# A two-layer hybrid decoder on one core: an SBUF pool for HGRN2's query and gate tiles, a smaller index branch, and pools that wait tile by tile

## The chip and the metric

The kernel runs on one core of a Trainium2 chip. The metric is device time in microseconds of one execution; of a set of runs the median counts. The engines, in the words of the profile: PE (TensorE, its weight loads as PEld), DVE (VectorE), ACT (ScalarE), POOL (GpSimd) and SP, which only issues DMAs. Each engine takes its instructions in a fixed order. On-chip memory is SBUF (128 partitions; a tile takes the same bytes in each) and PSUM (eight banks of 2 KB a partition, where matmuls accumulate).

## The reference

The input is `x` (512 tokens of 1024), a memory of 256 rows, and the weights of two layers in fp32. In each layer one projection of the normed residual (`w_in`) feeds four mixers side by side; their outputs, 256 columns each, go through `w_out` and are added to the residual. Then come cross attention to the memory and a SwiGLU FFN.

```
for l in range(2):
    h = rms_norm(x, norm_mix[l])
    c_hg, c_dsa, c_nsa, c_ml = split(h @ w_in[l])
    mixed = concat(hgrn2(c_hg), dsa(c_dsa), nsa(c_nsa), mlstm(c_ml))
    x = x + mixed @ w_out[l]
    x = x + cross_attention(rms_norm(x), rms_norm(mem))
    x = x + swiglu(rms_norm(x))
```

- HGRN2 takes queries `q`, forget gates `f`, values `i` and output gates `g` (four heads of 64) through a gated linear recurrence.
- DSA scores every key for every query with a small index branch: `score = sum over 8 heads of relu(iq . ik) * iw`. It keeps the 128 best keys of each query and attends to those with ordinary attention heads.
- NSA adds up three attentions (compressed blocks, selected blocks, a window), and mLSTM is a gated matrix memory, computed here in parallel form.

## The kernel before

**Order of the work.** All of a layer's code is emitted by Python generators. `weave` and `mix` (lines 1351 to 1367) take steps from several generators in turn, so that by the costs written in `COST` all end together; `first()` (line 245) marks instructions that go ahead of others. The program's framework then puts the instructions of each engine in an order that it chooses by a simulation of its own (line 1464), with the order of emission as the priority. So the code sets what may come early, not what does.

A layer has four stages:

1. `dsa_in` (line 538) multiplies the index columns of DSA while the residual is read row chunk by row chunk. Then `weave` runs DSA's index branch (`dsa`) beside a chain that holds `nsa_in`, `nsa`, `ml_in`, `ml`, `dsa_in2` and `hg_in`.
2. HGRN2 itself (`hg`), DSA's attention (`dsa_attn`), the projection out of the first mixers (`out_stage`) and the keys of the memory (`xa_kv`).
3. Cross attention (`xa_in`, `xa`).
4. The FFN.

**Products.** Each fp32 product is made of three: hi by hi, hi by lo, lo by hi. A weight tile is loaded by SP (`raw_tile`, line 265, three buffers `wr`), rounded to its hi on ACT (line 285) and its lo computed on POOL (line 286; six buffers each, `wh` and `wl`). `proj_T` (line 434) makes a transposed chunk of 128 columns by 512 tokens, 24 matmuls at lines 294 to 296, and evacuates it on DVE at line 438. `proj_tok` (line 441) makes blocks of 128 tokens by about 256 columns, 24 matmuls at lines 304 to 306 each, and evacuates each on ACT at line 450. Both accumulate in `acc`, two PSUM banks: a third accumulation can start only when one of the two has been evacuated.

**DSA's index branch** (lines 561 to 623). For the query blocks 1 to 3, `index(tb)` splits and transposes the queries into `iqs` and `iqT`, multiplies head by head (line 598), takes the ReLU on ACT (line 600) and adds the heads up in `iacc{tb}` on DVE (lines 603 to 607). `select(tb)` then runs 16 rounds of the eight largest and their replacement on DVE (lines 615 and 616) and writes a mask (line 619). `iqs` and `iqT` take turns in a tag of two buffers of 4 KB; each block has an `iacc` of its own.

**Pools.** Tiles live in pools, which are opened and closed like a stack, from the left and from the right of SBUF. A pool that lands on the bytes of a closed one waits for it: all its tiles wait for every user of every closed pool on those bytes. On the right lies `dsa`; when the index branch has been emitted, `hg_space` (line 687) closes it and opens `hgin` there, and `hg_in` (line 693) waits for that before it makes its tiles:

```
right.close()                                    # hg_space
self.hin = self.pool(right, "hgin", side="right")
while self.hin is None:                          # hg_in
    yield 0.5
pool = self.hin
self.h_q = self.t(pool, "h_q", [128, 2, S], bufs=1)
```

`hg_in` makes the transposed `h_q` and `h_f` (two chunks each, in the order q0, f0, q1, f1), then `h_v` and `h_g` (four blocks each). Right after, on the same side, comes `xk` with `memT`, pieces of the memory that SP loads (line 1166).

On the left lie, in the first stage, `keep` (what DSA keeps: masks, latent, queries), `ml` (mLSTM) and `nsa`. At the border to the second stage `ml` and `nsa` close, and on their bytes come the residual anew (`load_x`, `xT` from DRAM, lines 370 and following), `hg` with the tile `lvf` (line 740, first layer only), and `dat` with `wukv` (line 639), DSA's small weights. The PSUM banks besides `acc` are pools too (`ba`, `bb`, `bc` by stage).

Of the kernel before, what the change touches and what calls it, by code (L numbers as in the profile page):

```python
# [8 lines left out]
FR = mybir.dt.float32r  # L9
# [14 lines left out]
# column vectors, one column each, per layer  # L24
# [53 lines left out]
class Stream:  # L78
    """The layout of the weight stream: one flat array, tile after tile."""
# [6 lines left out]
    def tile(self, layer, name, kc, c0, c1):  # L86
        """Rows (kc chunks of 128) and columns c0:c1 of a weight -> [128, nk, c]."""
# [9 lines left out]
def pack(inp):  # L97
# [36 lines left out]
    # small weights: [w_uk | w_uv], w1 of the compressions, their w2  # L134
# [14 lines left out]
def plan(st, l):  # L149
    """Every tile of the stream of one layer in the order in which it is used."""  # L150
# [8 lines left out]
    # NSA without kc and vc  # L159
# [4 lines left out]
    tok_chunk("dsai", "w_in", DSA0 + 384, DSA0 + 680)  # L164
# [33 lines left out]
# rows of w_out by stage: HGRN2 0-1, DSA 2-3, NSA 4-5, mLSTM 6-7  # L198
# [4 lines left out]
class Kernel:  # L203
# [18 lines left out]
    # ---------------------------------------------------------------- helpers  # L222
    def psum(self, tag, shape=(128, 512), pool=None):
        """Banks by tag; the lane of a pool may have its own."""
        tag = self.alias.get(id(pool), {}).get(tag, tag)
        pool, bufs = self.pt[tag]
        return pool.tile(list(shape), FT, name=tag, tag=tag, bufs=bufs)

    def banks(self, stack, name, **tags):
        """The banks of a stage, besides those of acc."""  # L230
        pool = stack.enter_context(self.tc.tile_pool(name=f"{name}{self.l}", bufs=1, space=bass.MemoryType.PSUM))
        self.pt.update({t: (pool, n) for t, n in tags.items()})

    def t4(self, pool, name, shape, dt=FT):
        """A temporary of up to 4 KB a partition."""
        return pool.tile(list(shape), dt, name=name, tag="t4", bufs=self.nt[id(pool)][1])

    def t2(self, pool, name, shape, dt=FT):
        """A temporary of up to 2 KB a partition."""
# [5 lines left out]
    def first(self):  # L245
        """Scheduled ahead of what was emitted a while before."""
# [14 lines left out]
    def weights(self, key):  # L261
        """Loads the tiles of a chunk and splits them into hi and lo: a list by row chunk."""
        return [w for tile in self.plans[self.l][key] for w in self.weight_tile(tile)]

    def raw_tile(self, tile):
        """A tile of the stream [128, rows / 128, columns]."""
# [9 lines left out]
    def weight_tile(self, tile, pool=None):  # L276
        """Its hi and lo by row chunk; in a pool of their own if they are used for long."""
# [11 lines left out]
    def mm_T(self, acc, w, x):  # L289
        """acc[c, t] = w^T x; x by row chunk, as (hi, lo)."""  # L290
# [7 lines left out]
    def mm_tok(self, acc, w, x, tb, first=True, last=True):  # L298
        """acc[t, c] of one block of tokens."""
# [8 lines left out]
    def rsqrt(self, pool, dst, src, mul, add):  # L308
        """dst = (src * mul + add) ** -0.5, on small tiles."""
# [11 lines left out]
    def rope(self, x, c, s, half, pool, eng=None):  # L321
        """x [128, TB, H, d] in place; c, s [128, TB, 2 half]."""
# [11 lines left out]
    def sumsq(self, dst, x, pool):  # L334
        """dst [128, a(, b)] = sum of squares over the last axis of x."""
# [1133 lines left out]
```

## Time and profile before

| | |
|---|---|
| time, median of 3 runs | 1743.08 us (1739.02 to 1747.72) |
| the profiled execution, span from first to last instruction | 1744.4 us |
| PE busy | 1649.7 us, 95% |
| PEld busy | 1359.7 us, 78% |
| DVE busy | 993.2 us, 57% |
| POOL, ACT busy | 781.0 us, 712.0 us |
| mean granted clock of PE | 0.944 |

The profile gives no other time for its own execution than its span; the span lies within the runs' times. A matmul's busy time is modelled from its start to its end, and matmuls overlap, so a busy PE isn't a PE at its peak. The granted clock says at which speed PE ran: 1.00 is 2.4 GHz, 0.50 is 1.2 GHz, and a value between is a mean over a stretch. A wait names the work that ended last among what an instruction waited for. "Line" in the profile is a line of the kernel, often that of a helper, so that tiles say more than lines.

### The profile page before, as it was taken

How to read it: one execution, taken by the hardware profiler on the slowest of the kernel's cores; microseconds unless marked ns; L12 is line 12 of the kernel's file. 1: busy time of each engine (PE TensorE's matmuls, PEld its weight loads, DVE VectorE, ACT ScalarE, POOL GpSimd, SP SyncE). 2: the span in 40 equal slices, each digit the busy share in tenths (PEclk: the TensorE clock that was granted, in tenths of full speed). 3: DMA queues.
4: the chain of work that ended last, by engine and by line, in shares of the span. 5: the costliest groups of instructions: out<-in, count | busy, mean ns of one | idle time of the engine just before them, and what ended most of it. 6: DMA issues, size and time to landing. Idle time of an engine off the chain costs nothing.

```text
span 1744.4 us, 25033 instructions
## 1 busy us (share of the span) xinstructions
PE 1649.7 (95%) x9026; PEld 1359.7 (78%) x9030; DVE 993.2 (57%) x2022; ACT 712.0 (41%) x1537; POOL 781.0 (45%) x696
## 2 busy tenths in 40 slices
PE   7889899899899999999997998989998999999999
PEld 7778586677778888888896886867786888888887
DVE  5599856868774430343227997568867644214430
ACT  5455435326553322333334453452465433223321
POOL 5663232525615444444446543325464244444442
PEclk9999699959999999999998996988799999999999
DMA  5343111301503333333333321121022123333332
GB/s 155 103 117 84 37 43 37 100 13 35 171 13 97 92 93 95 96 97 91 98 96 109 95 83 43 43 75 43 22 84 84 43 91 94 89 101 96 92 101 67
DMA packets 82107, 140.38 MB, mean 80 GB/s; under 512 B 9400, under 2 KB 22456, under 8 KB 81984
## 3 DMA queue, kind: packets, MB, share of 16 engines
q1 hardware_dynamic: 79632, 133.81, 26.7%
q10 hardware_dynamic: 2032, 3.94, 0.7%
q8 instruction: 71, 1.16, 0.3%
q0 software_dynamic: 320, 1.05, 0.2%
q14 instruction: 52, 0.43, 0.1%
HBM read 134.55 MB, written 4.21 MB: 80 GB/s over the span
## 4 chain that ended last, share of the span: by engine, by line
PE 71%; DVE 19%; issue 3%; ACT 2%; POOL 2%; DMA 2%; SPq 0%; ACTq 0%; POOLq 0%; DVEq 0%
PE acc L294 12%; PE acc L295 12%; PE acc L296 12%; PE sc L295 5%; PE sc L296 5%; PE sc L294 5%; PE hb L770 3%; PE o L533 2%; DVE iacc L616 2%; PE tp L458 2%; DVE m L615 2%; PE acc L304 2%; PE acc L306 2%; PE acc L305 2%; PE mb L950 1%
## 5 line engine op out<-in xcount | busy, mean ns | idle before, releaser
L286 POOL TENSOR_TENSOR wl<-wr,wh 128x512 fp32r<-128x512 f32 (+4 forms) x496 | 623.6, 1265 | 658.0 <-ACT wh L285 624.3
L285 ACT ACTIVATE wh<-wr 128x512 fp32r<-128x512 f32 (+4 forms) x496 | 296.1, 603 | 517.4 <-PE acc L295 207.5
L294 PE MATMUL acc<-xh,wh 128*128 128x512 f32 (+1 forms) x704 | 275.6, 395 | 6.4 <-DVE xT L431 4.1
L295 PE MATMUL acc<-xl,wh 128*128 128x512 f32 (+1 forms) x704 | 274.9, 391 | 0.7 <-DVE xl L316 0.7
L296 PE MATMUL acc<-xh,wl 128*128 128x512 f32 (+1 forms) x704 | 273.8, 390 | 0.1
L431 DVE TENSOR_TENSOR xT<-acc,xT 128x512 f32<-128x512 f32 (+1 forms) x112 | 67.7, 610 | 215.8 <-PE acc L296 215.5
L294 PEld LDWEIGHTS acc<-xh,wh 128*128 128x128 f32 x704 | 133.9, 191 | 38.3 <-DVE xT L431 4.7
L295 PEld LDWEIGHTS acc<-xl,wh 128*128 128x128 f32 x704 | 134.6, 191 | 29.5 <-DVE xl L316 1.4
L296 PEld LDWEIGHTS acc<-xh,wl 128*128 128x128 f32 x704 | 134.3, 191 | 27.6 <-POOL wl L286 0.4
L304 PE MATMUL acc<-wh,xh 128*128 128x256 f32 (+2 forms) x480 | 138.0, 289 | 3.6 <-ACT h_g L450 1.3
L295 PE MATMUL sc<-xl,wh 128*128 128x512 f32 x352 | 139.6, 397 | 0.0
L296 PE MATMUL sc<-xh,wl 128*128 128x512 f32 x352 | 138.8, 394 | 0.0
L294 PE MATMUL sc<-xh,wh 128*128 128x512 f32 x352 | 138.4, 394 | 0.0
L296 PE MATMUL acc<-f_gh,wl 128*128 128x512 f32 x352 | 138.3, 395 | 0.0
L295 PE MATMUL acc<-f_gl,wh 128*128 128x512 f32 x352 | 138.1, 394 | 0.0
L294 PE MATMUL acc<-f_gh,wh 128*128 128x512 f32 x352 | 137.9, 394 | 0.0
L305 PE MATMUL acc<-wl,xh 128*128 128x256 f32 (+2 forms) x480 | 137.0, 286 | 0.0
L306 PE MATMUL acc<-wh,xl 128*128 128x256 f32 (+2 forms) x480 | 136.8, 285 | 0.0
L1329 DVE SCALAR_TENSOR_TENSOR f_b<-sc,R 128x512 f32<-128x512 f32 x44 | 30.4, 691 | 127.5 <-PE sc L296 127.5
L304 PEld LDWEIGHTS acc<-wh,xh 128*128 128x128 f32 x480 | 90.4, 189 | 6.3 <-ACT h_g L450 1.5
L305 PEld LDWEIGHTS acc<-wl,xh 128*128 128x128 f32 x480 | 90.6, 189 | 1.1 <-issue 0.6
L306 PEld LDWEIGHTS acc<-wh,xl 128*128 128x128 f32 x480 | 90.7, 189 | 0.9 <-issue 0.8
(396 smaller groups left out, 3204.4 us busy)
## 6 DMA issues: line engine op xcount, KB each, us to landing
wr<-in_wst SPq DMA_DIRECT2D x384, 256.0 KB, 2.6
wr<-in_wst SPq DMA_DIRECT2D x48, 128.0 KB, 2.6
wr<-in_wst SPq DMA_DIRECT2D x32, 192.0 KB, 2.4
wr<-in_wst SPq DMA_DIRECT2D x16, 262.0 KB, 2.7
wr<-in_wst SPq DMA_DIRECT2D x8, 296.0 KB, 3.4
wr<-in_wst SPq DMA_DIRECT2D x8, 264.0 KB, 2.8
m_Mb<-m_dram ACTq DMA_DIRECT2D x8, 256.0 KB, 3.5
memT<-in_memT SPq DMA_DIRECT2D x16, 128.0 KB, 2.1
```

The costliest lines, as they stand in the source:

```text
L285: nc.scalar.activation(hi, raw, AF.Copy)
L286: nc.gpsimd.tensor_tensor(lo, raw, hi.bitcast(FT), op=OP.subtract)
L294: self.nc.tensor.matmul(acc, wh, xh, start=(j == 0), stop=False)
L295: self.nc.tensor.matmul(acc, wh, xl, start=False, stop=False)
L296: self.nc.tensor.matmul(acc, wl, xh, start=False, stop=(j == n - 1))
L304: self.nc.tensor.matmul(acc, xh[:, s], wh, start=(first and j == 0), stop=False)
L305: self.nc.tensor.matmul(acc, xh[:, s], wl, start=False, stop=False)
L306: self.nc.tensor.matmul(acc, xl[:, s], wh, start=False, stop=(last and j == n - 1))
L431: self.nc.vector.tensor_add(self.xT[c][:, cols], acc, self.xT[c][:, cols])
L458: self.nc.tensor.transpose(p[:rows, j * 128:j * 128 + 128], src(j), self.ident)
L533: nc.tensor.matmul(o[64 * e:64 * e + 64, hp], v(sb), pT[e][:, sb * 128:sb * 128 + 128], start=(first and sb == 0), stop=(last and sb == tb ...
L770: nc.tensor.matmul(sc[s0:s1, b + t0:b + t1], kk[po:po + 64, b + s0:b + s1], qq[po:po + 64, b + t0:b + t1], start=True, stop=True)
```

## The change

- HGRN2's `h_q` and `h_f` get a pool `hgqf` of their own, opened on the right before `dsa`. `hg_in` makes them without waiting; it waits for `hgin`, which now holds `h_v` and `h_g` alone, after the four transposed chunks.
- `dsa` closes by a stack of its own (`index`).
- DSA's index branch has one `iqs`, one `iqT` and one `iacc` for all blocks. Its weights come in eight tiles of one row chunk instead of four of two, so that all weight buffers get smaller.
- Every pool that is opened by `pool`, by `banks` (PSUM), by `load_x` and by `open_sq` is opened with `reuse_waits="tile"`: a tile then waits only for the users of earlier tiles on its own bytes (in PSUM, its own bank), and not for all users of the closed pools.

Comments and docstrings that the diff takes out are left out here.

```diff
@@ plan
-    tok_chunk("dsai", "w_in", DSA0 + 384, DSA0 + 680)
+    out["dsai"] = [st.tile(l, "w_in", (k,), DSA0 + 384, DSA0 + 680) for k in range(8)]
@@ banks
-        pool = stack.enter_context(self.tc.tile_pool(name=f"{name}{self.l}", bufs=1, space=bass.MemoryType.PSUM))
+        pool = stack.enter_context(self.tc.tile_pool(name=f"{name}{self.l}", bufs=1, space=bass.MemoryType.PSUM, reuse_waits="tile"))
@@ load_x, and the same in open_sq
-        self.xp = self.xpool.enter_context(self.tc.tile_pool(name=f"xp{self.nx}", bufs=1))
+        self.xp = self.xpool.enter_context(self.tc.tile_pool(name=f"xp{self.nx}", bufs=1, reuse_waits="tile"))
@@ dsa_in
-                if c % 2 == 0:
-                    w += self.weight_tile(self.plans[self.l]["dsai"][c // 2])
+                w += self.weight_tile(self.plans[self.l]["dsai"][c])
@@ dsa, index(tb)
-            iqs = self.t4(pool, "iqs", [128, 8, 96], FR)
+            iqs = self.t(pool, "iqs", [128, 8, 96], FR, bufs=1)
...
-            iqT = self.t4(pool, "iqT", [128, 8, 128], FR)
+            iqT = self.t(pool, "iqT", [128, 8, 128], FR, bufs=1)
...
-            acc = self.t(pool, f"iacc{tb}", [128, n], bufs=1)
+            acc = self.t(pool, "iacc", [128, S], bufs=1)[:, :n]
@@ hg_space, hg_in
-    def hg_space(self, right):
-        right.close()
+    def hg_space(self, index, right):
+        index.close()
         self.hin = self.pool(right, "hgin", side="right")
...
-        while self.hin is None:
-            yield 0.5
-        pool = self.hin
+        pool = self.hqf
         self.h_q = self.t(pool, "h_q", [128, 2, S], bufs=1)
         self.h_f = self.t(pool, "h_f", [128, 2, S], bufs=1)
         for c in (0, 2, 1, 3):
             yield from self.proj_T(f"hgT{c}", (self.h_f if c > 1 else self.h_q)[:, c % 2], self.x)
...
+        while self.hin is None:
+            yield 0.5
+        pool = self.hin
         self.h_v = self.t(pool, "h_v", [128, TB, 256], bufs=1)
@@ pool
-        p = stack.enter_context(self.tc.tile_pool(name=f"{name}{self.l}", bufs=2, side=side))
+        p = stack.enter_context(self.tc.tile_pool(name=f"{name}{self.l}", bufs=2, side=side, reuse_waits="tile"))
@@ run
-            right = ExitStack()
+            right, index = ExitStack(), ExitStack()
+            self.hqf = self.pool(right, "hgqf", side="right")
...
-            pd = self.pool(right, "dsa", n2=4, n4=2, side="right")
+            pd = self.pool(index, "dsa", n2=4, n4=0, side="right")
...
-            self.weave((self.chain(self.dsa(pd, pk), self.hg_space(right)), COST["dsa"]),
+            self.weave((self.chain(self.dsa(pd, pk), self.hg_space(index, right)), COST["dsa"]),
```

## Rows read from the trace of the kernel before

**Rows 1.** Page, head and part 1: busy us, share of the span, instructions.

```profile
span 1744.4 us, 25033 instructions
...
PE 1649.7 (95%) x9026; PEld 1359.7 (78%) x9030; DVE 993.2 (57%) x2022; ACT 712.0 (41%) x1537; POOL 781.0 (45%) x696
```

**Rows 2.** Windows of the two stages: stretch, us, busy by engine, clock, DMA, GB/s.

```profile
181.00:215.20 34.20, 26.75 (x103) 19.05 (x101) 27.49 (x77) 13.24 (x41) 7.70 (x6) 0.55 0.11 32
215.20:302.00 86.80, 83.41 (x569) 66.91 (x570) 52.12 (x122) 42.67 (x108) 24.45 (x19) 0.96 0.15 43
302.00:318.40 16.40, 11.40 (x71) 8.29 (x69) 8.74 (x18) 6.66 (x13) 7.90 (x13) 0.96 0.51 169
1048.00:1077.30 29.30, 24.43 (x96) 17.81 (x95) 22.57 (x58) 9.76 (x31) 7.79 (x6) 0.55 0.15 45
1077.30:1174.10 96.80, 91.70 (x603) 73.28 (x602) 59.30 (x142) 47.17 (x118) 26.47 (x21) 0.92 0.17 48
1174.10:1183.00 8.90, 7.41 (x39) 6.37 (x39) 7.95 (x14) 4.50 (x9) 7.22 (x13) 0.69 0.32 119
```

**Rows 3.** Tiles: HGRN2's evacuations and DSA's masks, duration min/median/max, first and last start.

```profile
L438 DVE TENSOR_TENSOR h_q<-acc,R x2: 674/682/691, 215.2 to 226.6; 128x512 f32<-128x512 f32 x2
...
L450 ACT ACTIVATE h_v<-acc,r x4: 453/469/476, 240.7 to 257.5; 128x256 f32<-128x256 f32 x4
...
L450 ACT ACTIVATE h_g<-acc,rcol x4: 463/472/474, 267.5 to 277.3; 128x256 f32<-128x256 f32 x4
...
L619 DVE TENSOR_SCALAR dmask<-iacc x3: 344/412/1075, 107.4 to 214.3; 128x256 bf16<-128x256 f32 x1, 128x384 bf16<-128x384 f32 x1, 128x512 bf16<-128x512 f32 x1
...
L438 DVE TENSOR_TENSOR h_q<-acc,R x2: 680/686/691, 1077.2 to 1085.6; 128x512 f32<-128x512 f32 x2
```

**Rows 4.** Timeline of PE: start, us, instruction, [idle before <-releaser].

```profile
185.36 0.79 PE L950 MATMUL mb<-m_hi,m_hi 64*128 64x512 f32 x1 [4.09 <-ACT m_hi L919]
...
230.22 0.39 PE L295 MATMUL acc<-xl,wh 128*128 128x512 f32 x1
230.45 0.39 PE L296 MATMUL acc<-xh,wl 128*128 128x512 f32 x1
...
236.94 0.28 PE L304 MATMUL acc<-wh,xh 128*128 128x256 f32 x1
237.05 0.28 PE L305 MATMUL acc<-wl,xh 128*128 128x256 f32 x1
```

**Rows 5.** Windows of 10 us, columns as in rows 2.

```profile
150.00:160.00 10.00, 10.00 (x86) 9.60 (x85) 9.80 (x31) 5.77 (x12) 1.15 (x2) 1.00 0.07 26
290.00:300.00 10.00, 10.00 (x78) 7.30 (x72) 6.77 (x17) 6.68 (x18) 0.28 (x1) 1.00 0.01 2
610.00:620.00 10.00, 10.00 (x45) 8.10 (x44) 3.84 (x5) 3.62 (x6) 4.86 (x4) 1.00 0.37 98
1140.00:1150.00 10.00, 10.00 (x46) 8.07 (x44) 5.34 (x14) 3.31 (x10) 3.04 (x3) 0.50 0.10 33
```

**Rows 6.** Timeline of DVE: index scores of DSA's last block.

```profile
130.94 0.74 DVE L607 SCALAR_TENSOR_TENSOR iacc<-rel,d_idx,iacc 128x512 f32<-128x512 f32 x1
...
152.87 0.73 DVE L607 SCALAR_TENSOR_TENSOR iacc<-rel,d_idx,iacc 128x512 f32<-128x512 f32 x1
```

**Rows 7.** Chain at the ends of the first stages; a wait of PE.

```profile
309.76 6.67 DMA lvf<-in_levels
...
1174.14 3.62 DMA wukv<-in_wukv
...
PE acc L294 <- DVE xT L431: 3.4, 1, 3.4
```

**Rows 8.** Page, part 6: weight loads, KB each, median us to landing.

```profile
wr<-in_wst SPq DMA_DIRECT2D x8, 296.0 KB, 3.4
...
wr<-in_wst SPq DMA_DIRECT2D x48, 128.0 KB, 2.6
```

**Rows 9.** Waits of the SP queue, 150 to 260 us: total, times, longest.

```profile
SPq L1166 <- DVE dmask L619: 25.8, 1, 25.8
```

More of the change, by code (lines that the diff above doesn't have):

```diff
@@ L372, in open_sq @@
     def open_sq(self):
-        self.sq = self.xpool.enter_context(self.tc.tile_pool(name=f"sq{self.nx}", bufs=1))
+        self.sq = self.xpool.enter_context(self.tc.tile_pool(name=f"sq{self.nx}", bufs=1, reuse_waits="tile"))
     def layer_consts(self):
```

## The prediction

> **What bounds the kernel now.** I read the page first, for the one number that seems to close the case: the span is 1744.4 us and TensorE (PE) is busy for 95% of it [rows 1]. The profiled execution stands 1.3 us above the median of the runs, 1743.08 us; I make the sum against 1744.4, and this kernel's measurement can tell about 0.5% (8.7 us) from no change. PE's busy time is no proof of full work, since a matmul lasts longer at the lower clock, so I went next to the windows: where is PE busy at half speed? Of the whole kernel one kind of stretch stands out, once in each layer. In 181 to 215.2 us PE is busy 26.75 of 34.2 us at a mean granted clock of 0.55, that is mostly at 1.2 GHz; in 1048 to 1077.3 us it is 24.43 of 29.3 us at 0.55 [rows 2]. PE entered the first after 4.09 us of waiting [rows 4].
>
> Then the tiles, to see what ends the stretch. The last mask of DSA, the last reader of its index scores, starts at 214.3 us, and the first evacuation into `h_q` at 215.2 us; HGRN2's `h_v` follows from 240.7 and `h_g` from 267.5 us [rows 3]. The second layer repeats it: `h_q` first at 1077.2 us, where that stretch ends. The code says why. `hg_in` starts its projections only into tiles of the pool `hgin`, which lies on the bytes of the DSA pool and waits for all of that pool. Two transposed chunks are multiplied early into the two banks of `acc`; they can't leave, so no other projection can run, and PE has attention alone until the mask is done. VectorE (DVE) is not free then either: 27.49 of 34.2 us [rows 2].
>
> **The change, part by part.**
>
> *1. The transposed tiles get their own pool.* `h_q` and `h_f` no longer wait for DSA. Two chunks that now run after 215.2 us can run in the stretch: 2 x 24 matmuls at 0.23 us from start to start, 11.0 us [rows 4]. Behind them `hgi` and `hgg` have four blocks each, 24 matmuls at 0.12 us: 2.9 us a block. After the change `h_v` lies, by the sizes of the tiles in the code, on the index branch's `iqs` and `iqT`, and `h_g` mostly on `iqT` and `iacc`. With waits tile by tile `h_v` waits for the last index product (its scores end at 152.87 us [rows 6]), `h_g` still for the last mask. So four blocks of `hgi` (11.6 us) can leave, and two of `hgg` (5.8 us) can sit in the banks: 28.4 us of work for the stretch. The room there, as busy time at the granted clock: 34.2 - 26.75 x 0.55 = 19.5 us, and 29.3 - 24.43 x 0.55 = 15.9 us in the second layer; together 35.4 us. The supply holds: dense projections cost GpSimd 4.86 and ScalarE 3.62 per 10 us [rows 5], 16.6 and 12.4 us over the stretch, beside 7.70 and 13.24 of 34.2 already there [rows 2]. Does the freed time come off the end? The rest of the stage (215.2 to 302) is 83.41 of 86.8 us busy at 0.96, and its last ten microseconds before 300, with hardly a projection left, still have PE at 10.0 [rows 2, 5]. So the rest is bound by PE, and what leaves it shortens it. The bounds are 0 (the rest keeps its length) and 35.4. I take 30, near the upper end, because of those two rows; the deduction of 5 is one more fall of the clock like that of 1140 to 1150 us, ten microseconds at 0.50 [rows 5].
>
> The matmul's busy share would leave much less room (34.2 - 26.75 = 7.4 us in layer 0). The Trainium skill ("Perfetto Trace Analysis", Identifying the Most-Contended Engine) says that busy matmul time is a bad measure of headroom and puts the busy share of weight loads in its place. By that, as an estimate, the room is 34.2 - 19.05 / 0.81 = 10.7 us, the 0.81 being the share in a dense stretch, and 7.3 us in the second layer; the sum of this part would be 18 us and not 30. The trace agrees on the first half: busy share and clock differ as above.
>
> *2. Pools wait tile by tile.* At the first stage's end all tiles of the next wait for all of NSA and mLSTM. In layer 0 the chain then goes through the load of `lvf`, 6.67 us from 309.76, and PE waits 3.4 us for the residual; in layer 1 through the load of `wukv`, 3.62 us at 1174.14 [rows 7]. `wukv` lands on tiles of the compression that were done long before, so its wait goes: 3.6 us. Of the eight residual tiles the last lie on `m_tok`, which is read to the end, but no longer hold the others back: I take the 3.4 us. Room: 16.4 - 11.40 x 0.96 = 5.5 and 8.9 - 7.41 x 0.69 = 3.8 us [rows 2], so 0 to 9.3; I take 7. At the other borders the chain shows no wait for a pool: 0. The addresses of the PSUM banks change nothing but the same border.
>
> *3. One `iacc` instead of three.* The scores of a block now follow the selection before them. In layer 0 the last block's accumulation spread over 130.94 to 152.87 us, between the rounds of that selection [rows 6]; run after it, DSA can end up to 22 us later for each of two blocks. DSA's end is not the stage's: 214.3 + 44 = 258 us is still before 302. What hides it is NSA's and mLSTM's work on DVE, 9.80 of 10 us in 150 to 160 [rows 5]. Price 0. If that cover is gone, up to 22 us of DVE work moves into a rest of 86.8 - 19.5 = 67.3 us that holds 52.12 already [rows 2]: 74 us, 7 too many in each layer, 14 in all. That is the bound.
>
> *4. DSA's weights row chunk by row chunk.* Four loads of 296 KB become eight of half that, with four more splits on ScalarE and GpSimd; `iqs` and `iqT` alternated in two buffers and now have one each, which is the same order. A load of 128 KB takes 2.6 us to land against 3.4 [rows 8], so the fourth tile of layer 0 can be 2 us late, as three buffers now hold three row chunks and not six; the first product can be as much as 1.5 us earlier. Layer 1 has them under the FFN's dense PE. Price 0, bounds -1.5 and +2. The Trainium skill ("DMA: Bandwidth & Descriptors", Rules for kernel authors) advises to coalesce small transfers, which speaks against this part. The trace agrees in kind, with the two times to landing above, and gives it no more than those 2 us.
>
> Sum: 30 + 7 = 37 us; 1744.4 - 37 = 1707 us.
>
> **The rivals.**
>
> *The tail stays.* NSA and mLSTM are chains of dependent steps; if the rest is bound by them and not by PE, the projections move and the end does not. Against it: PE at 10.0 of 10 in 290 to 300 [rows 5]. For it: at this clock some of that is waiting inside the chain. Only part 2 is left: 1737 us.
>
> *DVE becomes the bound*, as worked out in part 3: 14 us given back, 1721 us.
>
> *Less room*: weight loads fill the stretch more than the clock lets one think, 18 us instead of 30: 1719 us, by the row of the weight loads [rows 2]. This is the rule of the Trainium skill named under part 1.
>
> *The borders give more.* The whole 35.4 and 9.3 us, and half of what the rests of the stages leave (86.8 - 83.41 x 0.96 = 6.7 and 96.8 - 91.70 x 0.92 = 12.4 us [rows 2]): 54 us, 1690 us.
>
> *Slower: a load blocks the weight queue.* SP issues in order. Today it stands 25.8 us at a load of `memT` that waits for DSA's mask [rows 9], with weights behind it, and nobody minds, since projections are stopped too. With finer waits such loads are placed earlier, into the time in which projections run at their densest. Six split tiles and three raw ones, about 2.8 us of PE each (12 matmuls x 0.23), cover 25 us; a stand of 45 us would cost 20 us of PE: 1764 us. It decides once the queue stands longer than those 25 us. Against it: the tiles under `memT` will be free when the index products end, long before the mask.
>
> *The change does not do what it says*: the order of the instructions is chosen by a scheduler, and if it keeps the projections where they are, the time stays at 1744 us.
>
> **How the numbers follow.** Forecast 0.48; tail stays 0.12; DVE 0.09; less room 0.05; borders give more 0.15; slower 0.07; not done 0.04. The predicted time is the forecast's, 1707 us. Faster by over 0.5% (below 1734.4): 0.48 + 0.09 + 0.05 + 0.15 = 0.77. Within 0.5%: 0.12 + 0.04 = 0.16. Slower: 0.07. The range runs from 1684, the deep case with a few microseconds of its own, to 1740, which takes in the staying tail; the queue's case, the unchanged one and the edges are left out, under 2 in 10.
>
> **What would show it.** Part 1: `h_q` and `h_f` evacuated in full before the last mask, `h_v` too, `h_g` just after it; the clock of that stretch near 1.0; the rest of the stage some 15 us shorter in each layer. Part 2: `lvf` and `wukv` gone from the chain. Part 3: the last mask later than 214 us, with the stage's end not following it. Part 4: the first weights in place earlier, dsa's products ending within 2 us of now. I am wrong if the stretch is filled and the stage ends where it did (the tail), if DVE is near 10 of 10 until the stage's end (part 3), or if SP shows waits of over 25 us with projections behind them.

## The result, and the profile after

The changed kernel takes 1724.93 us (median of 4 runs, 1717.81 to 1726.85), beside 1744.28 us for the kernel before in the same session: 19.4 us less, ratio 0.9896 with a 95% interval of 0.9866 to 0.9926. On a second chip it was 1726.21 against 1742.00 us, 0.9924 (0.9900 to 0.9947). It is faster, as forecast, by about half of the 37 us forecast. The profiled execution took 1724.88 us, with a span of 1723.1 us against 1744.4.

The head of the page and its part 1, against [rows 1]: TensorE (PE) is still at 95%.

```profile
span 1723.1 us, 25048 instructions
...
PE 1633.3 (95%) x9026; PEld 1347.7 (78%) x9030; DVE 989.5 (57%) x2022; ACT 712.8 (41%) x1545; POOL 793.5 (46%) x704
```

The evacuations and masks of layer 0 in the changed kernel, by tile, against [rows 3] (minimum, median and maximum duration in ns, then first and last start):

```profile
L438 DVE TENSOR_TENSOR h_q<-acc,R x2: 674/677/680, 179.2 to 193.4; 128x512 f32<-128x512 f32 x2
...
L450 ACT ACTIVATE h_v<-acc,r x4: 458/476/477, 206.6 to 219.2; 128x256 f32<-128x256 f32 x4
...
L450 ACT ACTIVATE h_g<-acc,rcol x4: 474/475/476, 224.5 to 240.3; 128x256 f32<-128x256 f32 x4
...
L618 DVE TENSOR_SCALAR dmask<-iacc x3: 294/351/406, 99.8 to 207.2; 128x256 bf16<-128x256 f32 x1, 128x384 bf16<-128x384 f32 x1, 128x512 bf16<-128x512 f32 x1
```

`h_q` leaves 36 us earlier than before, and the last projection is out at 240.3 us instead of 277.3. The stretch that stood at half clock is filled. But look at what comes behind it. These are windows of the changed kernel, with the columns of [rows 2] (stretch, its length, busy us of PE, weight loads, DVE, ACT and POOL, granted clock, DMA share, GB/s):

```profile
181.00:215.20 34.20, 33.85 (x214) 27.64 (x214) 31.24 (x83) 14.38 (x41) 13.48 (x11) 1.00 0.23 70
215.20:240.00 24.80, 24.80 (x187) 21.63 (x188) 14.37 (x37) 12.87 (x35) 6.92 (x6) 1.00 0.17 54
240.00:282.00 42.00, 33.03 (x154) 23.62 (x153) 26.73 (x57) 17.36 (x46) 11.78 (x9) 0.67 0.10 27
282.00:300.60 18.60, 17.47 (x137) 12.81 (x138) 11.29 (x33) 11.02 (x29) 2.59 (x4) 1.00 0.28 86
```

From 181 to 240 us PE is full at the upper of its two clocks (2.4 GHz). From 240, when the last projection is through, to 282 us it is at a mean of 0.67, and the windows of 10 us show how it falls: a short supply first, then half clock with PE called busy all the time.

```profile
230.00:240.00 10.00, 10.00 (x82) 8.89 (x81) 5.48 (x16) 5.35 (x14) 0.77 (x1) 1.00 0.01 2
240.00:250.00 10.00, 4.75 (x35) 3.13 (x34) 9.85 (x12) 5.99 (x15) 8.34 (x7) 0.99 0.40 111
250.00:260.00 10.00, 7.13 (x32) 5.10 (x32) 8.05 (x21) 4.55 (x12) 2.17 (x2) 0.66 0.00 0
260.00:270.00 10.00, 9.90 (x37) 6.52 (x37) 4.92 (x15) 4.34 (x13) 1.27 (x1) 0.51 0.01 2
270.00:280.00 10.00, 10.00 (x44) 7.85 (x44) 2.69 (x7) 1.82 (x5) 0.00 (x0) 0.50 0.00 0
...
1100.00:1110.00 10.00, 7.20 (x36) 4.87 (x36) 9.18 (x15) 6.20 (x15) 6.47 (x5) 0.66 0.38 111
1110.00:1120.00 10.00, 8.13 (x40) 4.75 (x40) 8.63 (x27) 7.16 (x20) 1.92 (x2) 0.84 0.00 1
```

The last two lines are about the same place in layer 1: its clock is on the way up again, at 0.84, in the second window, where layer 0 stays down for 20 us more.

For the account of the whole I cut the span into layer stages: the first stage (DSA's index, NSA, mLSTM and the projections in, to NSA's last output), the second part (HGRN2, DSA's attention, the products out and cross attention, to the next norm) and the FFN. In each, busy time times granted clock is the work at full clock, and the rest of the length I call *lost*. First the kernel before, then the changed one; the third and sixth pieces, the FFNs, lose next to nothing in either and are left out.

```profile
0.00:305.60 305.60, 269.84 (x1701) 227.84 (x1701) 220.15 (x542) 148.69 (x345) 133.10 (x116) 0.92 0.29 82
305.60:532.40 226.80, 209.28 (x1315) 171.95 (x1318) 167.07 (x357) 106.19 (x259) 103.31 (x113) 0.89 0.23 68
...
900.10:1174.10 274.00, 249.78 (x1550) 208.40 (x1548) 203.56 (x499) 129.53 (x309) 113.95 (x90) 0.90 0.25 71
1174.10:1392.40 218.30, 205.10 (x1314) 168.25 (x1317) 165.77 (x353) 105.36 (x259) 102.94 (x113) 0.91 0.20 58
```

```profile
0.00:300.60 300.60, 266.25 (x1702) 226.23 (x1703) 219.26 (x542) 149.07 (x349) 139.67 (x122) 0.94 0.30 89
300.60:524.50 223.90, 207.63 (x1314) 170.27 (x1316) 167.00 (x356) 105.90 (x259) 104.15 (x112) 0.90 0.21 59
...
892.60:1150.30 257.70, 237.00 (x1550) 198.44 (x1549) 202.55 (x499) 129.24 (x309) 117.19 (x92) 0.95 0.27 78
1150.30:1371.20 220.90, 206.37 (x1314) 169.56 (x1317) 164.69 (x355) 105.64 (x259) 103.24 (x112) 0.90 0.18 55
```

The lengths went from 305.6, 226.8, 274.0 and 218.3 us to 300.6, 223.9, 257.7 and 220.9 us: 5.0 and 2.9 us less, 16.3 less, and 2.6 us more. The work is the same (269.84 x 0.92 = 248 us and 266.25 x 0.94 = 250 in the first piece; the clock has two decimals, so such a product is good to a microsecond or two). So all that the change does is to the lost time: 305.6 - 248.3 = 57.3 us became 50.3 in layer 0's first stage, and 274.0 - 224.8 = 49.2 became 32.6 in layer 1's. Layer 0 is the riddle: 19.5 us were lost in its early stretch and are not any more, yet its stage is 5 us shorter. Even these 5 us are not the stretch's. The norm that the projections wait for writes its factor `R` earlier, first before, then after:

```profile
36.45 0.68 DVE L427 COPY R<-tp 128x512 f32<-128x512 f32 x1
```

```profile
30.14 0.69 DVE L427 COPY R<-tp 128x512 f32<-128x512 f32 x1 [4.78 <-PE tp L424]
```

From there on layer 0's first stage takes 270.5 us, against 269.1 before. The earlier norm goes with part 4's loads: it comes at 28.3 to 32.1 us in every run that has them, and at 35.8 to 37.0 in the three that have not (the kernel before, e2 and e8 below).

At the borders, the first 20 us behind each first stage, before and after:

```profile
305.60:325.60 20.00, 16.20 (x68) 12.50 (x69) 13.19 (x28) 8.01 (x15) 9.81 (x15) 0.83 0.47 152
1174.10:1194.10 20.00, 18.51 (x96) 15.25 (x96) 15.14 (x29) 6.66 (x13) 11.05 (x18) 0.74 0.15 54
```

```profile
300.60:320.60 20.00, 19.08 (x101) 14.74 (x101) 16.74 (x33) 9.04 (x17) 12.31 (x16) 1.00 0.28 83
1150.30:1170.30 20.00, 19.51 (x120) 15.58 (x121) 19.40 (x36) 7.33 (x15) 13.21 (x19) 1.00 0.17 54
```

Lost were 20 - 16.20 x 0.83 = 6.6 and 6.3 us; now 0.9 and 0.5. The loads of `lvf` and `wukv` [rows 7] are gone from the chain. The second parts as wholes, though, got 2.9 us shorter and 2.6 us longer, so these 11.5 us were all but given back further on.

### The profile page after: what moved, and what is told of

Its sections match the earlier page's. It is cut to its first block, busy times and chain, and to the rows that moved or that the text cites. A ratio compares the mean times of both kernels' runs of the same rounds, so it can differ in the third digit from the quotient of the medians.

```text
span 1723.1 us, 25048 instructions
## 1 busy us (share of the span) xinstructions
PE 1633.3 (95%) x9026; PEld 1347.7 (78%) x9030; DVE 989.5 (57%) x2022; ACT 712.8 (41%) x1545; POOL 793.5 (46%) x704
## 4 chain that ended last, share of the span: by engine, by line
PE 72%; DVE 14%; issue 6%; POOL 3%; DMA 3%; ACT 2%; SPq 0%; ACTq 0%; POOLq 0%; DVEq 0%
PE acc L295 11%; PE acc L296 11%; PE acc L294 11%; PE sc L295 5%; PE sc L296 5%; PE sc L294 5%; PE hb L770 3%; PE acc L304 3%; PE acc L306 3%; PE acc L305 3%; PE o L533 2%; DMA wr<-in_wst 2%; POOL wl L286 2%; PE tp L458 2%; PE mb L950 1%
## 5 line engine op out<-in xcount | busy, mean ns | idle before, releaser
L286 POOL TENSOR_TENSOR wl<-wr,wh 128x512 fp32r<-128x512 f32 (+5 forms) x504 | 633.4, 1265 | 627.2 <-ACT wh L285 589.4
L285 ACT ACTIVATE wh<-wr 128x512 fp32r<-128x512 f32 (+5 forms) x504 | 297.4, 597 | 508.0 <-PE acc L295 199.3
L294 PE MATMUL acc<-xh,wh 128*128 128x512 f32 (+1 forms) x704 | 271.3, 388 | 6.0 <-ACT wh L285 3.1
L431 DVE TENSOR_TENSOR xT<-acc,xT 128x512 f32<-128x512 f32 (+1 forms) x112 | 67.9, 611 | 214.3 <-PE acc L296 214.1
L296 PEld LDWEIGHTS acc<-xh,wl 128*128 128x128 f32 x704 | 132.3, 188 | 28.3 <-POOL wl L286 1.6
```

The lines of the kernel that those rows point to most:

```text
L285: nc.scalar.activation(hi, raw, AF.Copy)
L286: nc.gpsimd.tensor_tensor(lo, raw, hi.bitcast(FT), op=OP.subtract)
L294: self.nc.tensor.matmul(acc, wh, xh, start=(j == 0), stop=False)
L296: self.nc.tensor.matmul(acc, wl, xh, start=False, stop=(j == n - 1))
L431: self.nc.vector.tensor_add(self.xT[c][:, cols], acc, self.xT[c][:, cols])
```

## The experiments

Two theories were left by this profile. *Supply*: PE is the bound wherever independent products (projections, products out) are at hand; a hole opens where they have been used up, and moving them forward moves the hole. *Chain*: the tail of the stage takes its time in the dependent steps of NSA and mLSTM, whatever is beside it. A third, narrower one blamed the crowd at 240 us on VectorE and GpSimd.

### What the projections are worth

The first run leaves HGRN2's projections out of the changed kernel altogether (memsets in their place, so h_q, h_f, h_v and h_g hold 0.1):

```
-            yield from self.proj_T(f"hgT{c}", ..., self.x)
+            nc.gpsimd.memset(..., 0.1)
```

> The changed kernel without HGRN2's sixteen projection blocks of a layer: h_q, h_f, h_v and h_g are memset to 0.1, so what follows computes with those. Left out per layer: 96 matmuls at 0.23 us and 192 at 0.12 us, 45 us of PE. If the first stage is bound by PE (as the prediction had it), about 40 us per layer go: 1645 us. If it is bound by the chain of NSA and mLSTM, with the projections as mere filler, the stage keeps most of its length: 1700 to 1725 us, with PE at the lower clock for much of 180 to 290 us.

Measured (e3): 1671.32 us, ratio 0.9593 (0.9546 to 0.9639); against the changed kernel some 53 us less for 90 us of products, between the two numbers expected. The second leaves out of the kernel *before* the very products that step 1 of the prediction moves (memsets again, for two chunks, all of `h_v` and two blocks of `h_g`):

```
         for c in (0, 2, 1, 3):
+            if c % 2:
+                nc.gpsimd.memset((self.h_f if c > 1 else self.h_q)[:, 1], 0.1)
+                yield 5.2
+                continue
...
-        yield from self.proj_tok("hgi", ...)
-        yield from self.proj_tok("hgg", ...)
+        yield from self.proj_tok("hgg", ..., blocks=2)
```

> Kernel before without the very projections that part 1 of the prediction moves out of the rest of the stage (two transposed chunks, all four blocks of hgi, two of hgg; 28.4 us of TensorE in each layer; h_q, h_f, h_v, h_g filled with 0.1 there). If the rest is bound by TensorE, as step 1 said, each stage ends about 28 us earlier: 1688 us, ratio 0.968. If the rest is bound by the chain of NSA and mLSTM, the stages end 0 to 12 us earlier: 1720 to 1744. The changed kernel's gain of 5 us (layer 0) and 16 us (layer 1) would have the same unequal shares here if layers differ in the chain.

Measured (e8): 1701.67 us, 0.9763 (0.9719 to 0.9808). Its two first stages, same columns:

```profile
0.00:284.10 284.10, 244.11 (x1509) 203.47 (x1509) 213.02 (x538) 141.43 (x330) 124.29 (x115) 0.89 0.28 81
...
872.60:1127.70 255.10, 226.62 (x1357) 184.80 (x1356) 189.90 (x493) 122.53 (x294) 106.33 (x89) 0.86 0.23 64
```

The stages are 21.5 and 18.9 us shorter for 31 and 30 us of work taken out (248.3 - 244.11 x 0.89, 224.8 - 226.62 x 0.86). So what leaves the rest shortens it by about two thirds, in both layers alike; the lost time of the rest grows by the last third. This lies between the two theories' numbers, nearer to supply. It also shows that layer 0 could have gained as much as layer 1 from the leaving alone. What it did not get it lost in the placing: with the same products run by 240 us, the changed kernel's stage ends at 300.6 and not at 284.1 us.

### Which part of the change does it

Four runs take the change apart. Waits by pool instead of by tile in the changed kernel:

```
-... self.tc.tile_pool(..., reuse_waits="tile")
+... self.tc.tile_pool(...)
```

> The changed kernel, but every pool waits for all users of the closed pools again (no reuse_waits); own pool, one iacc and small weight tiles stay. If the pool of h_q and h_f carries the gain: two transposed chunks leave early, h_v and h_g wait for the last mask (about 207 us), 1728 to 1734 us. If the finer waits carry it: 1740 to 1745 us.

Measured (e1): 1733.78 us, 0.9951 (0.9928 to 0.9973). The tile waits alone in the kernel before, the reverse of that diff:

> The kernel before with nothing but reuse_waits=tile on the same four kinds of pools; layout, iacc and weight tiles as before. There h_q lies on ikT and iqs and h_f on iqs and iqT, which are free after the last index product (153 us), so if the finer waits are what frees the projections this alone gives the whole gain: 1722 to 1730 us, h_q evacuated at about 180 us. If the own pool is needed: 1738 to 1745 us, h_q still at 215 us.

Measured (e2): 1740.42 us, 0.9993 (0.9967 to 1.0018). The instructions of both pairs are the same ones in the same order on every engine, with fewer waits. `h_q` still leaves at 215.0 us in the second. So the finer waits give nothing alone and perhaps 0.3 to 0.5% together with the own pool. At the borders e2 does what part 2 said, here in the first 20 us behind each first stage:

```profile
305.80:325.80 20.00, 19.03 (x102) 14.73 (x102) 16.77 (x31) 9.08 (x17) 12.12 (x16) 1.00 0.27 83
1182.00:1202.00 20.00, 19.09 (x112) 15.87 (x112) 18.56 (x36) 7.71 (x15) 9.70 (x11) 0.91 0.10 27
```

It loses 1.0 and 2.6 us there (6.6 and 6.3 before). But e1, with the own pool and without the finer waits, loses only 2.6 and 0.9 by the same windows, though `lvf` and `wukv` are on its chain: beside the own pool the finer waits had little left to win there.

Then parts 3 and 4 alone, in the kernel before:

```
-    tok_chunk("dsai", "w_in", DSA0 + 384, DSA0 + 680)
+    out["dsai"] = [st.tile(l, "w_in", (k,), DSA0 + 384, DSA0 + 680) for k in range(8)]
...
-            acc = self.t(pool, f"iacc{tb}", [128, n], bufs=1)
+            acc = self.t(pool, "iacc", [128, S], bufs=1)[:, :n]
```

(and `iqs` and `iqT` with one buffer)

> Kernel before with parts 3 and 4 alone: one iacc, single iqs and iqT, DSA's weights row chunk by row chunk. The prediction's price for both is 0: 1744 us within 5, the last mask up to 44 us later than 214 us. The rival price is +14 us in two layers (1758). If the changed kernel's gain came from the earlier start of the chain, this one would show part of it: 1735 to 1740.

Measured (e7): 1729.51 us, 0.9921 (0.9877 to 0.9964), faster than the prediction's price of 0 allows, and than the 1735 to 1740 us of the other case. Part 4's loads alone, the first half of that diff:

> Kernel before with part 4's weight loads alone (eight of 148 KB instead of four of 296 KB). The prediction's price is 0, bounds -1.5 and +2 us: 1744 within 2. If the shrunk kernel's gain of about 15 us comes from the earlier first products, most of it is here: 1730 to 1738; otherwise it comes from the single buffers.

Measured (e11): 1735.37 us over 11 runs, 0.9960 (0.9939 to 0.9982): about 7 us, with the first stages no shorter in its profile (layer 0's ends at 307.7 us, against 305.6) and second parts of 218.5 and 213.5 us (226.8 and 218.3). And all but the own pool, with the changed kernel itself beside it on the same chip:

> Changed kernel without part 1: kernel before with one iacc, single iqs and iqT, DSA's weights row chunk by row chunk, and waits tile by tile; h_q and h_f still wait for DSA. If the own pool is what the change lives on (step 1 of the prediction), the time goes back to about 1728 us or more, the time of the shrunk kernel alone. If filling the early stretch only moves the hole, it is within 5 us of the changed kernel, 1719 to 1729.

> The changed kernel itself again, as the measure on this chip for the three others: ratio to the kernel before 0.987 to 0.992, span 1721 to 1726.

Measured (e9, and the changed kernel again): 1732.14 us, 0.9941 (0.9918 to 0.9964), and 1726.21 us, 0.9924 (0.9900 to 0.9947). The step on which the prediction put 30 of its 37 us, the own pool, is worth 6 us by the medians and 3 by the ratios, whose intervals overlap: that it is worth anything is barely shown, that it is not worth 30 is clear. Parts 2 to 4, priced at 7 us together, are worth 10 here. The windows of the two say where it goes. First the kernel without the own pool, then the changed one, second execution:

```profile
0.00:305.00 305.00, 275.23 (x1702) 232.53 (x1703) 211.39 (x540) 150.31 (x349) 137.63 (x119) 0.89 0.30 87
305.00:525.10 220.10, 204.74 (x1316) 167.68 (x1316) 169.23 (x359) 106.15 (x259) 107.62 (x114) 0.92 0.21 62
...
893.10:1166.60 273.50, 253.32 (x1549) 210.37 (x1548) 198.84 (x495) 130.49 (x308) 115.44 (x89) 0.88 0.25 71
1166.60:1383.10 216.50, 200.95 (x1316) 165.75 (x1317) 166.65 (x358) 106.14 (x260) 105.03 (x114) 0.92 0.20 58
```

```profile
0.00:298.50 298.50, 268.65 (x1702) 228.22 (x1703) 218.72 (x542) 149.17 (x349) 139.38 (x122) 0.92 0.30 90
298.50:525.90 227.40, 211.43 (x1316) 172.97 (x1317) 167.51 (x357) 105.80 (x259) 102.80 (x112) 0.89 0.20 58
...
893.90:1154.20 260.30, 240.30 (x1551) 201.20 (x1550) 202.56 (x499) 129.31 (x309) 117.58 (x92) 0.94 0.26 77
1154.20:1379.20 225.00, 210.62 (x1316) 172.60 (x1317) 163.95 (x354) 105.77 (x259) 104.53 (x112) 0.88 0.18 54
```

With the own pool the first stages are 6.5 and 13.2 us shorter, 19.7 in all (3.1 of the 6.5 lie in front of the first norm, at 31.4 and 28.3 us, where the own pool has no part yet); the second parts are 7.3 and 8.5 us *longer*, 15.8 in all. The difference of 3.9 us is that of the spans (1735.1 and 1731.1), to 0.1. Each is one execution, and both were slower than their medians. The second parts run the same products, and their work is 188 and 188, 185 and 185 us; what grows is the stretch at half clock that each has about 30 to 80 us in. The first 90 us of the second parts, first without the own pool, then with it:

```profile
305.00:395.00 90.00, 85.62 (x505) 68.31 (x504) 74.30 (x167) 32.31 (x83) 47.88 (x58) 0.85 0.16 48
1166.60:1256.60 90.00, 83.69 (x539) 67.02 (x539) 78.01 (x170) 32.87 (x90) 48.54 (x59) 0.85 0.15 46
```

```profile
298.50:388.50 90.00, 84.98 (x410) 67.73 (x411) 67.83 (x151) 25.35 (x64) 38.78 (x47) 0.75 0.14 39
1154.20:1244.20 90.00, 87.26 (x509) 68.90 (x509) 71.47 (x158) 28.31 (x76) 42.49 (x52) 0.75 0.12 35
```

### Is it the crowd on VectorE?

At 240 us DVE is full with 12 instructions. In its timeline the same operation takes 0.74 us while GpSimd is idle (14.76 us, until 239.23) and 1.64 us while GpSimd works beside it:

```profile
238.50 0.74 DVE L912 SCALAR_TENSOR_TENSOR m_y<-m_x,cols,m_y 128x512 f32<-128x512 f32 x1
...
248.15 1.64 DVE L912 SCALAR_TENSOR_TENSOR m_y<-m_x,cols,m_y 128x512 f32<-128x512 f32 x1
```

```profile
239.23 1.29 POOL L286 TENSOR_TENSOR wl<-wr,wh 128x512 fp32r<-128x512 f32 x1 [14.76 <-issue]
...
247.72 1.51 POOL L316 TENSOR_TENSOR m_lo<-m_th,m_hi 128x512 fp32r<-128x512 f32 x1 [1.29 <-ACT m_hi L919]
249.31 1.59 POOL L316 TENSOR_TENSOR m_Md<-m_Mb,kc 128x512 f32<-128x512 f32 x1
```

From 239.23 to 246.4 us GpSimd splits four weight chunks of the next stage (`wl`). The next run holds their loads back with a copy of one element that waits for NSA's third block:

```
+        if self.hold:
+            self.nc.scalar.activation(raw[0:1, 0, 0:1], self.mo[2][0:1, 0, 256:257], AF.Copy)
         with self.first():
             self.nc.sync.dma_start(raw...)
```

> Changed kernel with the loads of the next stage's first weights (wo0) held until NSA's third block is out, so GpSimd's four splits leave 239 to 246 us (and 1098 to 1107). Theory A (VectorE jammed by GpSimd empties TensorE there, and the clock falls behind it): TensorE busy over 8 of 10 in 240 to 250, the clock near 1.0 until 280, 8 to 20 us off the span, ratio 0.978 to 0.985. Theory B (the tail is NSA's and mLSTM's chain, whatever VectorE's neighbours do): 240 to 250 as before, time within 4 us of the changed kernel's, or some us more because the weights come later.

Measured (e5): 1717.09 us, 0.9848 (0.9792 to 0.9905).

```profile
240.00:250.00 10.00, 6.32 (x49) 4.25 (x48) 9.34 (x21) 6.97 (x19) 2.94 (x2) 1.00 0.00 0
250.00:260.00 10.00, 9.13 (x37) 5.73 (x38) 8.92 (x23) 5.75 (x16) 2.53 (x2) 0.69 0.01 2
260.00:270.00 10.00, 10.00 (x48) 7.85 (x46) 1.97 (x5) 2.32 (x6) 0.00 (x0) 0.50 0.00 0
270.00:280.00 10.00, 8.66 (x58) 5.75 (x54) 6.99 (x19) 7.83 (x24) 4.25 (x4) 0.95 0.27 83
```

DVE passes 21 instructions and not 12, but PE still runs short (6.32 of 10, not the 8 that theory A asked for) and the clock still falls, though it is back at 0.95 in 270 to 280 us (to fall once more behind that). Layer 0's first stage ends at 299.2 us (300.6) and layer 1's takes 261.7 (257.7). So the crowd makes the hole deeper, but it is not what makes the hole, nor the stage long. The time, at theory A's number, came another way: the gain lies where nothing was expected, in second parts of 219.8 and 218.7 us instead of 223.9 and 220.9 (one execution).

### Filling the hole

Work that is of no use, as a filler: four more score products, into a free bank, behind each of NSA's causal scores in its last two blocks.

```
+                if mask is None and tb >= 2 and self.dt_free:
+                    warm = self.psum("dt")
+                    for _ in range(HEAT):
+                        nc.tensor.matmul(warm[:, :n], q[0][:, h], kst[:, :n], ...)
```

> The changed kernel with four extra matmuls beside each score of NSA in query blocks 2 and 3 (the score's own operands, into the bank that DSA's index products no longer need; the result is not read): 64 per layer, about 13 us of PE at full clock. If the fall of the clock in 250 to 282 us holds the tail back: clock near 1.0 there and 8 to 15 us less, 1710 to 1717 us. If the tail waits on DVE and ACT whatever PE's clock: 1725 us. If PE is full: up to 26 us more, 1750 us.

Measured (e4): 1726.06 us, 0.9909 (0.9878 to 0.9940). In layer 0 the clock in 250 to 280 us is back at 0.87, 0.79 and 1.00, and the stage ends at 299.9 us: as early as without the 64 products more. The hole had room for them, and what the higher clock gave they took. Half of the 64 ran before 248 us and pushed the last `h_g` out from 240.3 to 248.7, so they filled the hole with projections, too. The number expected of a tail that waits on DVE and ACT, 1725 us, is the one that came; a filler that itself takes PE's time can't tell that case from the clock's. Layer 1, with less of a hole, paid for them: its stage takes 270.4 us instead of 257.7; and its second part, where the clock did not fall in this execution, 211.0 instead of 220.9.

A slower pace of the projections in the planner:

```
-..., "in": 93.0, ...
+..., "in": 60.0, ...
```

> Changed kernel with the pace of the projections (COST of 'in') at 60 instead of 93: the same work, HGRN2's projections emitted later beside NSA and mLSTM. If the tail is only short of filling (the clock's theory), projections move into 240 to 280 us, the clock there is near 1.0 and the span 5 to 15 us shorter; if the chain sets the stage, span within 5 us of 1723. Also shows how far a mere reordering moves the time.

Measured (e6): 1727.14 us, 0.9901 (0.9857 to 0.9946), 240 to 280 us as before: 0.74, 0.67, 0.50, 0.55. The products did not move: `h_g` leaves from 222.8 to 238.5 us (224.5 to 240.3). So the run leaves its question open; it looks as if the planner fills the early gaps first whatever the pace. Next they were held by a real dependency: `h_g` can't be written before NSA's second block has left (some 237 us).

```
+        for tb in range(TB):
+            nc.scalar.activation(self.h_g[0:1, tb, 0:1], self.mo[2][0:1, 0, 128:129], AF.Copy)
         yield from self.proj_tok("hgg", lambda tb: self.h_g[:, tb], 256, self.x)
```

> Changed kernel with h_g's evacuations held until NSA's second block has left (about 237 us), so two to four blocks of hgg (6 to 12 us of TensorE a layer) run behind 237 us instead of in front. If the lost TensorE time of the stage is conserved (the hole sits wherever the projections do not), span within 4 us of 1723, the hole at 215 to 240 us instead of 240 to 282. If a hole late in the stage is dearer than one before, 8 to 15 us faster.

Measured (e10): 1723.26 us, 0.9896 (0.9856 to 0.9936), no different from the changed kernel in time. In its profile layer 0's first stage takes 263.0 us from its norm (from 32.1 to 295.1 us) instead of 270.5 (30.1 to 300.6), layer 1's 260.5 instead of 257.7: some of the lost time is won back where most was lost. The hole did not move to 215 to 240 us, where PE is full; it stayed and got shorter, with the clock back at 1.00 in 270 to 280 us. Both holds together:

> Changed kernel with both holds: h_g's evacuations after NSA's second block (e10) and the next stage's first weights after its third (e5). If the supply of independent products decides, the two gains add: first stage of layer 0 as in e10 (7 us shorter), second stages as in e5 (219 to 221 us each instead of 221 to 227), span 1708 to 1715. If the chains decide, it is within 4 us of e5 or e10, 1717 to 1724.

Measured (e12): 1713.52 us, 0.9841 (0.9813 to 0.9868): the fastest version here; its interval ends where the changed kernel's begins in the one session (0.9866) and below it in the other (0.9900). It is not clear of e5, the late weights alone (0.9792 to 0.9905). Layer 0's first stage ends at 289.5 us and layer 1's takes 256.3 us; the second parts, 227.3 and 212.1 us, are not the 219 to 221 expected. One thing repeats: from its norm on, layer 0's first stage takes 263.0, 261.1 and 259.4 us in the three versions that hold `h_g` (e10, e12 and e13 below) and 269.7 to 270.6 us in the six that have its products in front (the changed kernel twice, e1, e4, e5, e6). So the place of these products alone is worth 7 to 11 us of that stage. In layer 1 the two groups overlap (256.1 to 260.5 and 256.7 to 270.4 us). Last, a hold for the second part, where five of the eight products out were kept from leaving until DSA's attention had ended its first block:

```
+            if s == 0 and c >= 3:
+                x1 = self.xT[c][0:1, 0:1]
+                self.nc.vector.scalar_tensor_tensor(x1, self.d_out[0][1][0:1, 0:1].bitcast(FT), 0.0, x1, op0=OP.mult, op1=OP.add)
             self.residual(c, acc)
```

> e12 with chunks 3 to 7 of the next stage's first products (wo0, about 14 us of TensorE a layer) kept in their banks until DSA's attention has ended its first block, some 64 us into the stage. If the half-clock stretch of the second stage (some 345 to 380 us) is only short of independent products, it ends sooner and the second stages take 208 to 216 us; if the lost time is conserved, the hole moves to 320 to 360 us and the second stages stay at 219 to 227.

Measured (e13): 1719.60 us, 0.9863 (0.9838 to 0.9889), not better than the former; the second parts take 230.0 and 222.2 us. There the hole only moved forward (layer 0's clock is at 0.50 in 320 to 360 us, in e12 in 340 to 370), as expected for lost time that is conserved. Holding more back is no cure there.

## Why the prediction was right, and where it was wrong

**The stretch: right, to its size.** It was to take 19.5 us of work in layer 0. It took 33.85 x 1.00 - 26.75 x 0.55 = 19.1 us at full clock, and `h_v` and two blocks of `h_g` were out by 229 us. The rival *less room* fails with it, though its 1719 us lie nearer to the result than the forecast. The measure that the Trainium skill gives ("Perfetto Trace Analysis", Identifying the Most-Contended Engine) had put the room at 10.7 us; the trace disagrees, since weight loads, too, are longer at half clock: those of 128x128 fp32 took 333 ns (median) in this stretch before and 188 ns in it after. Their busy share told of the clock and not only of the work.

**The failed step: "So the rest is bound by PE, and what leaves it shortens it."** The rest was to be some 15 us shorter in each layer. In layer 0, to NSA's last output, it was 90.4 us long (215.2 to 305.6 us) and is 85.4 (215.2 to 300.6), and the norm in front of it came 6.3 us earlier. Two things stood in the place of that step. Taking the products out shortens a stage by two thirds of their time only (e8: 21.5 and 18.9 us for some 30). And putting them in front costs the chain: in layer 0 all of that went again, counted from the norm (269.1 us before, 247.1 in e8, 270.5 now). NSA's last two blocks and mLSTM's last two heads, left alone from 240 us, run short, and the clock falls to half behind that. That the placing does it shows in the runs that hold `h_g`, with 7 to 11 us less. The row that misled, PE at 10.0 in 290 to 300 us [rows 5], is a row of the kernel before with the projections just gone; ten microseconds were too short a look at what the tail does without them, and the deduction of 5 us for "one more fall of the clock" was the right thought at a quarter of its size: 42 - 33.03 x 0.67 = 19.9 us are lost in 240 to 282. The rival *the tail stays* described layer 0, not layer 1, where the clock fell less far. The rival of DVE as the bound named 1721 us and was near by luck: DVE is not near 10 of 10 until the stage's end, but at 4.92 and 2.69 in 260 to 280 us.

**A second gap in the same term: the sum ended with the stage.** Part 1's 30 us were counted as if nothing behind the stage could answer. The prediction saw one kind of half-clock stretch in the whole kernel; the kernel before has another in its second part (350 to 390 us, at 0.53):

```profile
350.00:390.00 40.00, 39.16 (x167) 31.98 (x168) 24.44 (x64) 8.53 (x29) 11.28 (x15) 0.53 0.03 7
```

Between e9 and the changed kernel beside it, where only part 1 differs, the first stages gave 19.7 us and the second parts took 15.8 back. Against the kernel before this does not show so plainly, because with parts 2 to 4 alone the second parts were shorter (226.8 and 218.3 us before, 220.1 and 216.5 in e9, one execution each); that is where most of those parts' 9 us of span lie. The growth sits in the second part's half-clock stretch. What sets its length is not settled: it was shorter when the next stage's weights came late (e5) and not when the products themselves were held (e13).

**Half of the sum came, and much of that by luck.** Of the 16 to 19 us that came, the own pool, with 30 of the forecast's 37, brought 3 to 6. Some 10 came from parts 2 to 4, and part 4, priced at 0, has about 7 by itself (e11).

**Part 2: the mechanism right, the sum given back.** 7 us was the term, and 5.7 + 5.8 us less are lost at the two borders, in windows a little longer than those of the bound of 9.3. Part 2 alone brings 5.6 + 3.7 us of it (e2), and over the whole kernel it is worth nothing alone.

**Part 3: price not settled.** The last mask was to come later than 214.3 us; it comes at 207.2, earlier by about as much as the norm. With parts 3 and 4 alone it is at 216.9 us (e7), but so it is, at 217.8, with part 4 alone (e11): no delay of part 3's own shows. Parts 3 and 4 together measured 0.9921 (e7) and part 4 alone 0.9960 (e11); the intervals overlap, so no run shows whether part 3 is worth 0 or some 7 us.

**Part 4: price 0 with a bound of -1.5 us; measured -0.4%, about 7 us** (e11), outside the bound. Nor did it cost anything to go against the rule to coalesce small transfers (the Trainium skill, "DMA: Bandwidth & Descriptors", Rules for kernel authors, which speaks of mostly overhead under 64 KB): the 148 KB loads land in 2.2 us, the 296 KB ones took 3.4 [rows 8]. Where the 7 us arise isn't settled; e11's profile shows the first norm 4.6 us earlier (31.9 us, not 36.5), not an earlier end of that stage, and shorter second parts.

**The slower rival** had its stand: SP waits 45.0 us in one piece, at the load of `xT`, for mLSTM's products (the waits of the SP queue, 150 to 300 us: total, times, longest). This is the very length that it named as harmful. No harm of it shows: no projection of that stage was left to load, and eight weight loads had gone out between 217.96 and 246.8 us, before it. No run was made to test it.

```profile
SPq L370 <- PE mb L950: 45.0, 1, 45.0
```

## What to carry to other kernels

A half-clock stretch tells how much work fits into it, not what the end gains: ask what the place that the work comes from will look like without it, and take the work out there (as e8 does) before counting on the gain. Independent products are a stock that keeps PE full beside dependent chains; here the planner spent them early, and a real dependency that held some back for the last gap made layer 0's first stage 7 to 11 us shorter. In the whole time that shows only together with the later weights (e12, about 10 us); alone the hold changed nothing (e10). Add up lost time (length less busy times clock) over all stages, also those that the change doesn't touch.

## What the hardware showed that was not expected

The granted clock can stay at half for 20 us while PE counts as busy throughout: 9.90 and 10.00 of 10 at 0.51 and 0.50 in 260 to 280 us, behind a window with 4.75 of 10. With fillers of no use (e4) the same place was at 0.79 and 1.00.

VectorE's operation on 128x512 took 0.74 us at 238.50, with GpSimd idle, and 1.64 us at 248.15, all but wholly beside GpSimd's operations on tiles of that size. That stretch cost little here, as e5 shows.

One execution differs from another by such a fall: the fastest version ran in 1706.84 to 1717.65 us, and the profile of the 1706.84 has layer 1's second part at a clock of 0.97 and a length of 212.1 us, where that of the changed kernel has 0.90 and 220.9. So the lengths of the second parts, one execution each, are less sure than the medians; that they grow with the own pool in layer 1 shows in five executions with it and with no weights of the next stage held (220.9 to 225.5 us; a sixth, with the fillers, has 211.0; e3, without the projections, is left out with 232.6) against six without it (213.5 to 219.2). In layer 0 the two groups overlap (223.9 to 227.4 with it, 218.5 to 233.3 without).
